# A two-layer mixture-of-experts model on one core: the router multiplies the residual itself, and the norm's scale moves into the router's matrix

## The chip, the cores and the metric

The kernel runs on one core of one Trainium2 chip. The metric is the device time of one launch in microseconds, the median of several executions; less is better.

## The reference, cut to what matters

There are two layers. In each, 256 tokens `x` and 256 context tokens `xc` (width 1024) go through a token mixer and then through a hierarchical mixture of 32 experts. The second layer computes the context only as far as the mixer of `x` needs it, so its experts see 256 tokens, the first layer's 512.

```
mod = c_act @ w_mod[i] + b_mod[i]
sh1, sc1, g1, sh2, sc2, g2 = split(mod, 6)
x = x + g1 * mix
x = x + g2 * hierarchical_moe(rms_norm(x, norm2_g) * (1 + sc2) + sh2, ...)

def hierarchical_moe(t, ...):
    group_p, group_idx = top_k(softmax(t @ w_group + b_group), 1)
    sel_logits = (t @ w_expert + b_expert)[the 8 experts of that group]
    top_val, top_idx = top_k(sel_logits, 2)
    top_w = softmax(top_val) * group_p
    y = sum over the two experts of top_w * (silu(t @ w1[e]) * (t @ w3[e])) @ w2[e]
```

`rms_norm(x, g)` is `x * rsqrt(mean(x*x) + 1e-6) * g`. The group's 4 logits and the experts' 32 are one product of width 36.

## The kernel before

Tokens lie in tiles of 128 rows: four in layer 0 (two sides, `x` and `xc`, of two tiles each), two in layer 1. Each layer runs `mixers`, whose last product is `mix` (matmuls `pmix`, three passes of split operands; DVE multiplies by the gate, `prm`/`prl`, and adds to the residual `x`), and then `moe` (L1442 on).

**Router.** For each tile `moe` squares `x` on ACT with a sum (`sq`), DVE makes `rnv`, POOL takes the power -1/2 (`rn`, L347), DVE multiplies and adds (`h = x*rn*G2 + sh2`, two passes of 1024 columns), POOL writes `h` to DRAM (`h2d`, L1461), PE transposes `h` in two groups of four (`pth`, L1466), ACT copies them (`h2T`). For each pair of tiles PE makes the logits (`plg`, 16 fp32 matmuls) and turns them back (`plt`, L1482), and DVE adds the bias (`lg`).

```
for i, t in enumerate(tiles):
    r = self.square(tp, self.x[t // 2][:, t % 2])
    self.stt(h, self.x[t // 2][:, t % 2], r, self.G2[t // 2], OP.mult, OP.mult)
    self.add(h, h, self.sh2[t // 2])
    self.G.dma_start(hd[i * 128:(i + 1) * 128], h)
```

`route` then ranks on DVE in some fifty small operations, with one round of small matmuls (`prk`) that counts the tokens of each expert. In `experts`, `look` multiplies one-hot rows by token numbers (`pvi`), `place` makes addresses (`ix`, `at`), and `fetch` gathers the token rows of a quad of four experts from `h2d` with an indirect DMA issued by POOL (`xg`, L1741). `count` makes the number of tokens that overflow a slot (`k`), which DVE loads into a register for the branch at L1972 and L1973 (`If(v > done)`, not entered for these inputs). The tiles of `route`, `weigh` and `learn` come from the experts' pool `ep`, which takes the memory of the router's own tiles.

**Experts.** 32 experts in 8 quads. Of a quad, `gather` transposes the fetched rows (`pgt`, L226), `first` multiplies by W1 and W3 (`pab`), `hidden` makes silu and product and transposes (`pat`), `second` multiplies by W2 in two column halves (`pye`, then ACT and DVE split the result, `yy`), and `combine` adds back to the tokens (`pcb`, then DVE `pg`, L195, and `x`, L198). Each quad needs 12 weight pieces of 1 MB, loaded by SP's queue (L340); 9 are loaded ahead in layer 0 and 16 in layer 1, the others as buffers come free. While a quad is in `hidden` and `second`, steps of the quad before's `combine` and of the next quad's `gather` lie between, at places set in the loop from L1999 on. `self.line` chains PE's matmuls in the order written.

**The next layer's modulation.** `mod_steps` multiplies the activations by eight 1 MB pieces of `w_mod` (`pm`, four matmuls for each piece, three buffers), adds the bias (`w<-w,pm`), transposes (`ptm`) and copies (`modT`). For layer 1 the first of its three parts runs inside layer 0's router, eight steps ahead of the routing's matmuls.

Elsewhere each engine's order is that of a scheduler that follows the program's order and the operations' readiness.

Of the kernel before, what the change touches and what calls it, by code (L numbers as in the profile page):

```python
# [19 lines left out]
D = 1024  # L20
# [157 lines left out]
class Net:  # L178
    def __init__(self, tc, A, out, dbg=None, stop=None):
        self.tc, self.nc, self.A, self.out = tc, tc.nc, A, out  # L180
        self.dbg, self.stop = dbg, stop
        self.line = None
        self.V, self.S, self.G, self.T, self.Y = (tc.nc.vector, tc.nc.scalar, tc.nc.gpsimd, tc.nc.tensor,
                                                  tc.nc.sync)
# [43 lines left out]
    def queue(self, i):  # L228

        if self.line is not None:  # L230
            ins = getattr(i, "ins", i)
            for last in self.line:
                self.tc.add_manual_dep(ins, last.name, mybir.DependencyInfo(mybir.DependencyClass.NoSync,
                                                                            mybir.DependencyReason.DATA), reason="line")
            self.line = [ins]
        return i

    def mm3(self, o, lh, ll, rh, rl, start, stop):
# [46 lines left out]
    def consts(self):  # L285
# [37 lines left out]
        self.bg = None  # L323
        self.modT = [cp.tile([128, 16, 2], F32, name=f"modT{l}") for l in range(L)]
        self.dmod = [self.dp.tile([2, 128, 512], F32, name=f"dmod{l}") for l in range(L)]

# [24 lines left out]
    def mod_steps(self, l, b):  # L351

        pm = self.pm(name="pm")
        for k in range(8):
            w = self.weight(self.A["wmod"][l, b, k])
            for q in range(4):
                self.mm(pm[32 * q:32 * q + 32, :], self.actp[:, k, :], w[:, q * 512:(q + 1) * 512], k == 0, k == 7,
                        tile_position=(0, 32 * q))
            if k < 7:
                yield  # L360
        w = self.slot()
        bt, R, nt = w[:, 0:512], w[:, 512:1024], w[0:64, 1024:1536]
# [4 lines left out]
        self.add(R, bt, pm)  # L367
        if b == 0:
            pt = self.ax(name="ptm")
            for j in range(4):  # L370
                self.T.transpose(pt[:, j * 128:(j + 1) * 128], R[:, j * 128:(j + 1) * 128], self.ident)
            mT = self.modT[l]
            pv = pt.rearrange("p (j q s) -> p q j s", j=4, q=4)[:, :, :, 0:2]
            mq = mT.rearrange("p (q j) s -> p q j s", q=4)
            self.V.tensor_copy(mq[:, 0:2], pv[:, 0:2])
            n1 = self.P["n1"].rearrange("p (l q j) -> p l q j", l=L, q=2)[:, l]
            self.stt(mq[:, 2:4, :, 0], pv[:, 2:4, :, 0], 1.0, n1, OP.add, OP.mult)
            self.stt(mq[:, 2:4, :, 1], pv[:, 2:4, :, 1], 1.0, n1, OP.add, OP.mult)
        else:
# [5 lines left out]
            self.G.dma_start(self.dmod[l][b - 1], R)  # L385
        yield

# [1026 lines left out]
    def moe_open(self, l):  # L1414
# [21 lines left out]
        self.V.tensor_copy(self.tri, self.cst["tri"])  # L1436
        ss = range(self.T0 // 256, 2)
        self.G2 = {s: self.vec(self.rb, l, "G2", s, tag="rb") for s in ss}
        self.sh2 = {s: self.vec(self.rb, l, "sh2", s, tag="rb") for s in ss}

    def moe(self, l):
# [6 lines left out]
        with ExitStack() as cx:  # L1448
# [4 lines left out]
            with tc.tile_pool(name=f"rl{l}", bufs=2, reuse_waits="tile") as tp:  # L1453
                hs, hTs, lT = [], [], None
                for i, t in enumerate(tiles):
                    r = self.square(tp, self.x[t // 2][:, t % 2])
                    h = tp.tile([128, D], F32, name="h2", bufs=NT)
                    self.stt(h, self.x[t // 2][:, t % 2], r, self.G2[t // 2], OP.mult, OP.mult)
                    self.add(h, h, self.sh2[t // 2])
                    hs.append(h)  # L1460
                    self.G.dma_start(hd[i * 128:(i + 1) * 128], h)  # L1461
                    hT = tp.tile([128, 8, 128], F32, name="h2T", bufs=3)
                    for kh in range(2):
                        pt = self.ax(name="pth2")
                        for k in range(4):
                            self.T.transpose(pt[:, k * 128:(k + 1) * 128],  # L1466
                                             h[:, (4 * kh + k) * 128:(4 * kh + k + 1) * 128], self.ident)
                        self.copy(hT[:, 4 * kh:4 * kh + 4], pt.rearrange("p (k t) -> p k t", k=4))
                    hTs.append(hT)
                    if i % 2 == 0:  # L1470
                        lT = tp.tile([128, 128], F32, name="lT")
# [3 lines left out]
                    for k in range(8):  # L1475
                        for u in range(2):
                            self.mm(pl[64 * u:64 * u + 36, 0:128], self.wr[:, k], hTs[i - 1 + u][:, k], k == 0, k == 7,
                                    tile_position=(0, 64 * u))
# [19 lines left out]
    def route(self, rp, l, lg, NT, R):  # L1498
# [39 lines left out]
        Mf = M[1:]  # L1538
        pk = self.ax(name="prk")
        H = PARTS[l]  # L1540
        hn = NT // H
# [128 lines left out]
    def experts(self, l, ep, R, more, later, hd, NT, NTOK, tiles):  # L1670
# [40 lines left out]
        def place(qd, v):  # L1711
# [6 lines left out]
            g["at"] = ep.tile([128, nb], I32, name="at")  # L1718
            self.add(g["at"], g["ix"], e)

# [123 lines left out]

        def first(qd):

# [3 lines left out]
            for k in range(8):  # L1850
# [7 lines left out]
                for b in range(g["nb"]):  # L1858
                    for e in range(n):
                        self.mm(ps[b][32 * e:32 * e + 32], g["xT"][k // 4][:, k % 4, b, e], w[e], k == 0, k == 7,  # L1860
                                tile_position=(0, 32 * e))

        def hidden(qd):
# [33 lines left out]
        def second(qd):  # L1897
# [4 lines left out]
            for hf in range(2):  # L1902
# [5 lines left out]
                for b in range(g["nb"]):  # L1908
                    ws = g["ws"][:, b:b + 1]
                    py = self.sx(name="pye")[0:n]  # L1910
                    for c in range(2):
# [7 lines left out]
                    g["y"][hf, b] = yy  # L1919
                yield  # L1920

# [37 lines left out]

        self.line = []  # L1960
        for qd in range(2):
            prepare(qd)
            place(qd, look(qd, self.tok4, 4, "pvi")[:, :, 0])
            if qd == 0:
                fetch(0)
                go(later)
        more(ep)
        self.line = None
# [22 lines left out]
        first(0)  # L1991
        self.learn(ep, NT, R)
        if not self.last:
            self.spread(ep, l, NT, R, "sm")
        for qd in range(2):
            worth(qd, look(qd, R["val"][:, :, qd, 4:12], 8, "pvw"))
        ex = none()
        for qd in range(nq):
# [4 lines left out]
            if qd + 2 < nq:  # L2003
                prepare(qd + 2)
            if qd > 0:
# [5 lines left out]
            com = combine(*([qd - 1] + (["x"] if qd - 1 == x_at else []))) if qd > 0 else none()  # L2011
            gat = gather(qd + 1) if qd + 1 < nq else none()
# [14 lines left out]
            out = second(qd)  # L2027
            go(out, 1)
            xout = second("x") if qd == x_at else none()
# [59 lines left out]
```

## Time and profile before

| | us |
|---|---|
| median of 3 runs | 1653.12 |
| lowest, highest | 1651.6, 1655.12 |
| the profiled run's own time | 1651.6 |
| its span, first to last instruction | 1649.7 |
| PE busy | 1493.0 (91%) |
| DVE busy | 959.2 (58%) |
| ACT busy | 534.6 (32%) |
| POOL busy | 83.7 (5%) |
| mean granted clock of TensorE | 0.964 |
| moved from HBM | 380.81 MB, 239 GB/s over the span |

PE, DVE, ACT and POOL are the engines for matmuls, vectors, activations and the rest; SP issues the weight loads. "Idle before, <- X" in a row is the time an engine stood before an instruction and what released it. PE's fp32 matmuls are recorded as two passes, so 16 of them show as x32; transposes show once. Granted clock 1.00 is 2.4 GHz and 0.50 is 1.2 GHz.

### The profile page before, as it was taken

The page shows a single profiled execution, that of the slowest core. Times are in us where ns is not written, and L with a number is a line of the kernel's source. Part 1 is how long each engine was busy: PE and PEld are TensorE (multiplying, and loading weights), DVE is VectorE, ACT ScalarE, POOL GpSimd, SP SyncE. Part 2 cuts the span into 40 slices and gives each one's busy share as a digit, 9 for nine tenths or more (in the row PEclk, how much of TensorE's full clock was granted, in tenths as well). Part 3 has the DMA queues.
Part 4 walks back from the last instruction along what each step waited for, and adds up shares of the span by engine and source line. Part 5 has one row for each costly group of instructions (what it writes and reads, how often), then busy time and mean ns, then how long its engine had stood idle before and what let it go on. Part 6 is the DMA issues. An engine that isn't in the chain of part 4 may idle for free.

```text
span 1649.7 us, 26481 instructions
## 1 busy us (share of the span) xinstructions
PE 1493.0 (91%) x10595; PEld 969.3 (59%) x10595; DVE 959.2 (58%) x2252; ACT 534.6 (32%) x1044; POOL 83.7 (5%) x110
## 2 busy tenths in 40 slices
PE   4899999999998999699979989999999995998885
PEld 2566755687886797344444446686889893333221
DVE  7788997655475554445343466696576753233324
ACT  3423434342253322022111224244455531222211
POOL 1000000000000001101000000000000102000000
PEclk9899999999999999799989998999999997999998
DMA  7533254431221497899999954548624388999995
GB/s 284 191 117 130 93 204 147 165 138 52 89 91 52 135 342 255 275 387 386 386 339 392 387 208 180 209 165 304 214 78 154 92 291 310 373 381 382 379 380 194
DMA packets 147772, 384.81 MB, mean 233 GB/s; under 512 B 10167, under 2 KB 15863, under 8 KB 135612
## 3 DMA queue, kind: packets, MB, share of 16 engines
q1 hardware_dynamic: 140204, 367.65, 61.7%
q0 software_dynamic: 6864, 13.06, 2.4%
q10 hardware_dynamic: 576, 2.36, 0.5%
q8 instruction: 85, 1.39, 0.3%
q14 instruction: 43, 0.35, 0.1%
HBM read 380.81 MB, written 12.81 MB: 239 GB/s over the span
## 4 chain that ended last, share of the span: by engine, by line
PE 35%; DVE 8%; DMA 7%; issue 4%; ACT 3%; SPq 1%; POOL 1%; POOLq 0%; DVEq 0%; ACTq 0%
PE pab L223 9%; PE pye L223 7%; PE pcm L223 6%; PE pcb L223 4%; DMA w<-in_w_dram 4%; PE pbr L223 1%; PE pgt L226 1%; DVE wl L201 1%; DVE zz L209 1%; PE pmix L223 1%; ACT xT L215 1%; DMA w<-in_winc_dram 1%; PE pm L223 1%; PE po L223 1%; ACT wh L215 1%
## 5 line engine op out<-in xcount | busy, mean ns | idle before, releaser
L223 PE MATMUL pcm<-hh,wh 128*128 128x512 f32 (+1 forms) x736 | 262.4, 357 | 2.7 <-ACT wh L215 2.7
L223 PE MATMUL pcm<-hh,wl 128*128 128x512 f32 (+1 forms) x736 | 257.6, 351 | 1.6 <-DVE wl L201 1.6
L223 PE MATMUL pcm<-hl,wh 128*128 128x512 f32 (+1 forms) x736 | 258.7, 352 | 0.2 <-DVE hl L201 0.2
L223 PE MATMUL pab<-w,xT 128*32 128x512 f32 x2048 | 230.6, 594 | 19.9 <-DMA w<-in_w_dram 19.8
L201 DVE TENSOR_TENSOR wl<-w,wh 128x1024 fp32r<-128x1024 f32 x128 | 155.5, 1222 | 127.0 <-ACT wh L215 120.8
L215 ACT ACTIVATE wh<-w 128x1024 fp32r<-128x1024 f32 x128 | 134.5, 1057 | 246.9 <-PE pcm L223 164.5
L223 PEld LDWEIGHTS pab<-w,xT 128*32 128x32 f32 x2048 | 63.6, 110 | 181.6 <-issue 134.6
L223 PEld LDWEIGHTS pcm<-hh,wh 128*128 128x128 f32 x736 | 140.9, 192 | 35.1 <-issue 10.2
L223 PEld LDWEIGHTS pcm<-hh,wl 128*128 128x128 f32 x736 | 140.4, 191 | 22.3 <-issue 4.8
L223 PEld LDWEIGHTS pcm<-hl,wh 128*128 128x128 f32 x736 | 140.9, 191 | 18.3 <-issue 2.9
L209 DVE SCALAR_TENSOR_TENSOR th<-th,pab 128x256 f32<-128x256 f32 (+1 forms) x33 | 13.9, 421 | 233.2 <-ACT th L212 233.2
L223 PE MATMUL pye<-w,aT 128*32 128x512 f32 x1024 | 119.8, 609 | 3.5 <-ACT xT L215 3.5
L223 PE MATMUL pcb<-yy,oT 128*128 128x512 f32 x320 | 95.3, 426 | 3.1 <-DVE pg L195 1.6
L212 ACT ACTIVATE th<-pab 128x256 f32<-128x256 f32 (+1 forms) x33 | 12.6, 383 | 237.9 <-PE pab L223 229.4
L209 DVE SCALAR_TENSOR_TENSOR yy<-pye,ws,yy 128x512 fp32r<-128x512 f32 x64 | 48.0, 750 | 65.5 <-ACT yy L212 65.4
L223 PE MATMUL ptk<-wh,hh 128*128 128x256 f32 x288 | 82.8, 287 | 0.0
L223 PE MATMUL ptk<-wh,hl 128*128 128x256 f32 x288 | 82.7, 287 | 0.0
L223 PE MATMUL ptk<-wl,hh 128*128 128x256 f32 x288 | 82.3, 286 | 0.0
L223 PEld LDWEIGHTS pcb<-yy,oT 128*128 128x128 f32 x320 | 56.8, 194 | 42.4 <-issue 16.9
L212 ACT ACTIVATE yy<-pye,ws 128x512 fp32r<-128x512 f32 x64 | 44.0, 687 | 114.1 <-PE pye L223 114.1
L223 PE MATMUL pm<-w,actp 128*32 128x512 f32 x384 | 72.1, 625 | 6.2 <-DMA w<-in_wmod_dram 6.2
L195 DVE TENSOR_TENSOR pg<-g,pcb 128x512 f32<-128x512 f32 x96 | 64.8, 684 | 21.5 <-PE pcb L223 20.0
(405 smaller groups left out, 2535.9 us busy)
## 6 DMA issues: line engine op xcount, KB each, us to landing
w<-in_w_dram SPq DMA_DIRECT2D x198, 1024.0 KB
w<-in_wmod_dram SPq DMA_DIRECT2D x48, 1024.0 KB
w<-in_winc_dram SPq DMA_DIRECT2D x42, 1024.0 KB
w<-in_wint_dram SPq DMA_DIRECT2D x10, 1024.0 KB
w<-in_wout_dram SPq DMA_DIRECT2D x10, 1024.0 KB
w<-in_wmix_dram SPq DMA_DIRECT2D x8, 1024.0 KB
dtb<-T SPq DMA_DIRECT2D x4, 1472.0 KB
T<-dtb SPq DMA_DIRECT2D x4, 1472.0 KB
```

Of the source, the lines that this page charges most:

```text
L195: return self.V.tensor_tensor(o, a, b, op=OP.mult)
L201: return self.V.tensor_tensor(o, a, b, op=OP.subtract)
L209: return self.V.scalar_tensor_tensor(o, a, s, b, op0=op0, op1=op1)
L212: return self.S.activation(o, a, f, bias=bias, scale=scale, **k)
L215: return self.S.activation(o, a, AF.Copy, bias=0.0, scale=1.0)
L223: return self.queue(self.T.matmul(o, l, r, start=start, stop=stop, **k))
L226: return self.queue(self.T.transpose(o, a, ident))
```

## The change

Six things are done; line numbers after are those of the new file.

1. The router's transposes (`pth`, now L1501) take `x`. The norm's scale is multiplied into the router's matrix (`wrg`, one DVE operation for each side), the shift's product with the matrix becomes a bias (`brs`, 8 fp32 matmuls `pbs` for each side), and the logits are `plt * rs + brs`, one DVE operation for each tile. `h` is still made and written to `h2d`, after the transposes.
2. The squares are in two parts of 768 and 256 columns, and POOL's power writes the scale directly.
3. `mod_steps` transposes the other two parts of the modulation also (`modX`: four transposes and a copy each, twice a layer).
4. `route`, `learn` and `spread` take their tiles from the router's pool. The branch, which is not entered, now also copies the values that `learn` and `tables` read onto themselves, so their operations come behind it. Seven steps of the next layer's modulation stand ahead of `route` and the eighth behind it; the bias is added after the first `at` (`follow`).
5. In the last quad, the steps of quad 6's `combine` stand between the pieces of `first`; `second` yields after each half block, its second half lies in other PSUM buffers (`self.acc`), and the last `combine` is spread over it.
6. By the scheduler's choice, in the passage from layer 0 to layer 1 ACT's and DVE's splits of the first weight pieces (`wh`, `wl`, two each) stand ahead of the squares of the next norm.

```diff
+        for s in ss:
+            self.wrg[s] = ro.tile([128, 8, 36], F32, name=f"wrg{s}")
+            self.mul(self.wrg[s], self.wr, self.modX[l][:, 1, :, s:s + 1].to_broadcast([128, 8, 36]))
+            pb = self.ax(name="pbs")
+            for k in range(8):
+                self.mm(pb[:, 0:36], self.modX[l][:, 0, k, s:s + 1].to_broadcast([128, 128]), self.wr[:, k], k == 0, k == 7)
+            self.brs[s] = ro.tile([128, 36], F32, name=f"brs{s}")
+            self.add(self.brs[s], self.br, pb[:, 0:36])
...
-                    r = self.square(tp, self.x[t // 2][:, t % 2])
-                    h = tp.tile([128, D], F32, name="h2", bufs=NT)
-                    self.stt(h, self.x[t // 2][:, t % 2], r, self.G2[t // 2], OP.mult, OP.mult)
-                    self.add(h, h, self.sh2[t // 2])
-                    hs.append(h)
-                    self.G.dma_start(hd[i * 128:(i + 1) * 128], h)
+                    self.act(sq[:, 768:], x[:, 768:], AF.Square, accum_out=ss[:, 1, c])
+                    self.ts(ms[:, 1, c], ss[:, 1, c], 1.0 / D, ms[:, 0, c], OP.mult, OP.add)
+                    self.G.tensor_tensor(rs[:, c], ms[:, 1, c], self.mhalf[:, 0:1], op=OP.pow)
...
                             self.T.transpose(pt[:, k * 128:(k + 1) * 128],
-                                             h[:, (4 * kh + k) * 128:(4 * kh + k + 1) * 128], self.ident)
+                                             x[:, (4 * kh + k) * 128:(4 * kh + k + 1) * 128], self.ident)
...
-                    self.add(lg[:, i - 1:i + 1], pl[:, 0:128].rearrange("p (u e) -> p u e", u=2)[:, :, 0:36],
-                             self.br.rearrange("p (o e) -> p o e", o=1).to_broadcast([128, 2, 36]))
+                    for u in range(2):
+                        j = i - 1 + u
+                        self.stt(lg[:, j], pl[:, 64 * u:64 * u + 36], rs[:, j:j + 1], self.brs[t // 2], OP.mult, OP.add)
...
-            R = {"tok": self.cst["tok"]}
-            more = self.route(rp, l, lg, NT, R)
+            R = {"tok": self.cst["tok"], "pool": rp}
             later = iter(())
             if l + 1 < L:
                 later = self.mod_steps(l + 1, 0)
-                for _ in range(8):
+                for _ in range(7):
                     next(later)
+            more = self.route(rp, l, lg, NT, R)
+            next(later, None)
...
-        more(ep)
+        more(R["pool"])
...
+            for v1 in (R["w"], R["rk"], R["upto"], gb[0]["ix"], gb[1]["ix"]):
+                self.V.tensor_copy(v1, v1)
...
-                first(qd)
+                first(qd, com if qd + 1 == nq else ())
...
-            last = combine(qd) if qd + 1 == nq else none()
-            go(last, NT)
+            last = none()
+            if qd + 1 == nq:
+                last = combine(qd)
+                go(out, 1)
+                go(last, 2)
```

PE's order in layer 0's router, before, from the first step of the modulation behind the mixer (`pm`, four matmuls for each piece) on:

```order
2468 L223 MATMUL pm<-w,actp 32x512 x12
2469 L1466 MATMUL pth_5930<-ident,h_5925 128x128 x4
2470 L1466 MATMUL pth_5936<-ident,h_5925 128x128 x4
2471 L223 MATMUL pm<-w,actp 32x512
2472 L1466 MATMUL pth_5956<-ident,h_5951 128x128 x4
2473 L1466 MATMUL pth_5962<-ident,h_5951 128x128 x4
2474 L223 MATMUL plg<-h2T,wr 36x128 x16
2475 L223 MATMUL pm<-w,actp 32x512 x4
2476 L1482 MATMUL plt<-ident,lT 128x128
```

The same place now:

```order
2473 L1501 MATMUL pth_5978<-ident,x_5401 128x128 x4
2474 L1501 MATMUL pth_5984<-ident,x_5401 128x128 x4
2475 L1501 MATMUL pth_6001<-ident,x_5401 128x128 x4
2476 L1501 MATMUL pth_6007<-ident,x_5401 128x128 x4
2477 L223 MATMUL pm<-w,actp 32x512 x9
2478 L223 MATMUL plg<-h2T,wrg_5432 36x128
2479 L223 MATMUL pm<-w,actp 32x512 x3
2480 L223 MATMUL plg<-h2T,wrg_5432 36x128 x15
2481 L1501 MATMUL pth_6045<-ident,x_5402 128x128 x4
2482 L223 MATMUL pm<-w,actp 32x512
2483 L1521 MATMUL plt<-ident,lT 128x128
```

The transposes of the first pair went ahead of the modulation's first three pieces. Of the 32 matmuls `pm`, 29 stood ahead of the counting matmuls `prk` before, and 28 do now.

DVE's order in layer 1 between the second address of the first quads and the branch, before (`lt`, `val`: the routing weights; `oT`: one-hot rows for `combine`; `k`: the overflow):

```order
1850 L198 TENSOR_TENSOR at<-ix,none 128x2
1851 L195 TENSOR_TENSOR lt_13540<-r_13124,s_13236 128x64
1852 L198 TENSOR_TENSOR k_13212<-k_13210 128x32
1853 L205 TENSOR_SCALAR oT<-c_iota,ix 128x128
1854 L206 TENSOR_SCALAR k_13212<-k_13212 128x32
1855 L198 TENSOR_TENSOR lt_13539<-lt_13539,lt_13540 128x64
1856 L205 TENSOR_SCALAR k_13212<-k_13212 128x32
1857 L205 TENSOR_SCALAR oT<-c_iota,ix 128x128
1858 L205 TENSOR_SCALAR k_13212<-k_13212 128x32
1859 L1631 CAST val<-lt_13539 128x16x4
1860 L205 TENSOR_SCALAR oT<-c_iota,ix 128x128
```

The same place now:

```order
1867 L198 TENSOR_TENSOR at<-ix,none 128x2
1868 L198 TENSOR_TENSOR k_13291<-k_13289 128x32
1869 L206 TENSOR_SCALAR k_13291<-k_13291 128x32
1870 L205 TENSOR_SCALAR k_13291<-k_13291 128x32 x2
1871 L1631 SCALAR_TENSOR_TENSOR k_13298<-k_13296,k_13291 128x32
1872 L1633 CAST k_13300<-k_13298 128x1
1873 L2015 TENSOR_LOAD k_13300
1874 L2016 COMPARE_AND_BRANCH
```

Only the overflow's operations are left between the address and the branch; the others went behind it. Layer 0 has the same with more of them.

PE's order at the end of layer 1, from the last quad's first products (`pab`) on, before:

```order
4831 L223 MATMUL pab<-w,xT 32x512 x64
4832 L223 MATMUL pcb<-yy,oT 128x512 x2
4833 L226 MATMUL pat<-ident,th 128x128 x4
4834 L223 MATMUL pcb<-yy,oT 128x512 x2
4835 L223 MATMUL pye<-w,aT 32x512 x16
4836 L223 MATMUL pcb<-yy,oT 128x512 x8
4837 L223 MATMUL pye<-w,aT 32x512 x16
4838 L223 MATMUL pcb<-yy,oT 128x512 x4
```

The same place now:

```order
4853 L223 MATMUL pab<-w,xT 32x512 x8
4854 L223 MATMUL pcb<-yy,oT 128x512 x2
4855 L223 MATMUL pab<-w,xT 32x512 x8
4856 L223 MATMUL pcb<-yy,oT 128x512 x2
4857 L223 MATMUL pab<-w,xT 32x512 x32
4858 L226 MATMUL pat<-ident,th 128x128 x4
4859 L223 MATMUL pye<-w,aT 32x512 x24
4860 L223 MATMUL pcb<-yy,oT 128x512 x4
4861 L223 MATMUL pye<-w,aT 32x512 x8
4862 L223 MATMUL pcb<-yy,oT 128x512 x4
```

The eight `pcb` of the quad before went between the first products, and four of the last eight went ahead of the last `pye`.

## Rows read from the trace of the kernel before

**Rows 1.** The page's chain that ended last: share of the span by engine.

```profile
PE 35%; DVE 8%; DMA 7%; issue 4%; ACT 3%; SPq 1%; POOL 1%; POOLq 0%; DVEq 0%; ACTq 0%
```

**Rows 2.** Chain of waits, layer 1's router: start us, us, what.

```profile
1364.24 1.16 ACT sq L212 x2
...
1370.65 1.23 DVE h L198
...
1372.17 7.35 DMA h2d<-h
...
1388.80 5.01 DMA xg<-h2d,at
...
1395.89 13.11 PE pab L223 x120
```

**Rows 3.** Timeline of DVE, layer 1's router: start us, us, instruction [idle before].

```profile
1377.64 0.23 DVE L198 TENSOR_TENSOR lg<-plt,br 128x72 f32<-128x72 f32 x1 [5.76 <-PE plt L1482]
1379.65 0.09 DVE L1587 MEMSET k<- 128x32 f32 x1 [1.78 <-DMA h2d<-h]
...
1386.45 0.15 DVE L198 TENSOR_TENSOR at<-ix,none 128x2 int32<-128x2 f32 x1
```

**Rows 4.** Timeline of PE, layer 1: the mixer's end and the logits.

```profile
1350.99 0.39 PE L223 MATMUL pmix<-wl,mh 128*128 128x256 f32 x1 [2.60 <-DVE wl L201]
...
1373.89 2.70 PE L223 MATMUL plg<-h2T,wr 128*36 128x128 f32 x32
```

**Rows 5.** Windows, layer 1: us, busy PE, PEld, DVE, ACT, POOL, granted clock, DMA share, GB/s.

```profile
1385.00:1405.00 20.00, 14.14 (x110) 6.88 (x114) 3.40 (x26) 2.39 (x4) 4.10 (x4) 0.73 0.67 210
...
1500.00:1600.00 100.00, 83.49 (x684) 27.35 (x688) 31.62 (x67) 20.04 (x37) 4.88 (x5) 1.00 1.04 380
```

**Rows 6.** Timeline of PE, layer 0's router.

```profile
639.71 2.78 PE L223 MATMUL pm<-w,actp 128*32 128x512 f32 x24
644.84 1.77 PE L1466 MATMUL pth<-ident,h 128*128 128x128 f32 x8 [2.35 <-DVE h L198]
...
661.38 1.28 PE L223 MATMUL pm<-w,actp 128*32 128x512 f32 x8 [2.17 <-DMA w<-in_wmod_dram]
665.85 1.92 PE L223 MATMUL pm<-w,actp 128*32 128x512 f32 x2 [3.18 <-DMA w<-in_wmod_dram]
...
671.25 0.58 PE L223 MATMUL pvi<-tok,oh 128*128 128x4 f32 x4 [1.72 <-DVE oh L192]
...
681.78 3.81 PE L226 MATMUL pgt<-ident,xg 128*128 128x128 f32 x16 [6.47 <-DVEq L1973]
```

**Rows 7.** Timeline of DVE, layer 0's router.

```profile
660.61 0.09 DVE L1587 MEMSET k<- 128x32 f32 x1 [2.12 <-DMA h2d<-h]
...
669.81 0.69 DVE L198 TENSOR_TENSOR w<-w,pm 128x512 f32<-128x512 f32 x1 [1.01 <-DMA w<-in_bmod_dram]
```

**Rows 8.** Timeline of POOL, layer 0's router: the first gather.

```profile
674.19 1.10 POOL L1741 DMA_INDIRECT xg<-h2d,at  x1 [10.20 <-DVE oh L192]
```

**Rows 9.** Windows, layer 0, same columns as rows 5.

```profile
675.00:690.00 15.00, 8.53 (x61) 4.56 (x65) 8.69 (x44) 2.39 (x4) 3.87 (x4) 0.63 0.49 161
```

**Rows 10.** Chain of waits, layer 0's first quad: fp32 matmuls with a 128-column stationary operand.

```profile
699.66 1.88 PE pvw L223 x16
```

**Rows 11.** Timeline of PE, the end of layer 1.

```profile
1619.11 1.92 PE L223 MATMUL pab<-w,xT 128*32 128x512 f32 x16 [0.80 <-DMA w<-in_w_dram]
...
1623.82 3.64 PE L223 MATMUL pye<-w,aT 128*32 128x512 f32 x32
...
1631.49 5.31 PE L223 MATMUL pye<-w,aT 128*32 128x512 f32 x32
...
1638.90 0.51 PE L223 MATMUL pcb<-yy,oT 128*128 128x512 f32 x1 [0.79 <-DVE yy L209]
```

**Rows 12.** Timelines of PE and ACT, from layer 0 to layer 1.

```profile
986.94 1.11 PE L549 MATMUL pth<-ident,xn 128*128 128x128 f32 x4 [3.51 <-DVE rnv L206]
...
988.66 1.99 ACT L215 ACTIVATE wh<-w 128x1024 fp32r<-128x1024 f32 x2
```

More of the change, by code (lines that the diff above doesn't have):

```diff
@@ L181, in __init__ @@
         self.dbg, self.stop = dbg, stop
-        self.line = None
+        self.line, self.behind = None, None
         self.V, self.S, self.G, self.T, self.Y = (tc.nc.vector, tc.nc.scalar, tc.nc.gpsimd, tc.nc.tensor,
@@ L236, in queue, with follow @@
         return i
+    def follow(self, i, last):
+        self.tc.add_manual_dep(getattr(i, "ins", i), getattr(last, "ins", last).name,
+                               mybir.DependencyInfo(mybir.DependencyClass.NoSync, mybir.DependencyReason.DATA),
+                               reason="behind")
     def mm3(self, o, lh, ll, rh, rl, start, stop):
@@ L324, in consts @@
         self.modT = [cp.tile([128, 16, 2], F32, name=f"modT{l}") for l in range(L)]
+        self.modX = [cp.tile([128, 2, 8, 2], F32, name=f"modX{l}") for l in range(L)]
         self.dmod = [self.dp.tile([2, 128, 512], F32, name=f"dmod{l}") for l in range(L)]
@@ L366, in mod_steps @@
             yield
-        self.add(R, bt, pm)
+        i = self.add(R, bt, pm)
+        if self.behind is not None:
+            self.follow(i, self.behind)
+            self.behind = None
         if b == 0:
@@ L385, in mod_steps @@
             self.G.dma_start(self.dmod[l][b - 1], R)
+            pt = self.ax(name="ptm")
+            for j in range(4):
+                self.T.transpose(pt[:, j * 128:(j + 1) * 128], R[:, j * 128:(j + 1) * 128], self.ident)
+            pv = pt.rearrange("p (j q s) -> p q j s", j=4, q=4)[:, :, :, 0:2]
+            self.V.tensor_copy(self.modX[l][:, b - 1].rearrange("p (q j) s -> p q j s", q=2),
+                               pv[:, 2:4] if b == 1 else pv[:, 0:2])
         yield
@@ L1453, in moe @@
             with tc.tile_pool(name=f"rl{l}", bufs=2, reuse_waits="tile") as tp:
-                hs, hTs, lT = [], [], None
+                ss = tp.tile([128, 2, NT], F32, name="ss", bufs=1)
+                ms = tp.tile([128, 2, NT], F32, name="ms", bufs=1)
+                rs = tp.tile([128, NT], F32, name="rs", bufs=1)
+                early = slice(0, 768)
                 for i, t in enumerate(tiles):
-                    r = self.square(tp, self.x[t // 2][:, t % 2])
-                    h = tp.tile([128, D], F32, name="h2", bufs=NT)
-                    self.stt(h, self.x[t // 2][:, t % 2], r, self.G2[t // 2], OP.mult, OP.mult)
-                    self.add(h, h, self.sh2[t // 2])
-                    hs.append(h)
-                    self.G.dma_start(hd[i * 128:(i + 1) * 128], h)
+                    sq = tp.tile([128, D], F32, name="sq")
+                    self.act(sq[:, early], self.x[t // 2][:, t % 2, early], AF.Square, accum_out=ss[:, 0, i:i + 1])
+                    self.ts(ms[:, 0, i:i + 1], ss[:, 0, i:i + 1], 1.0 / D, EPS, OP.mult, OP.add)
+                hTs, lT = [], None
+                for i, t in enumerate(tiles):
+                    x = self.x[t // 2][:, t % 2]
+                    c = slice(i, i + 1)
+                    sq = tp.tile([128, D], F32, name="sq")
+                    self.act(sq[:, 768:], x[:, 768:], AF.Square, accum_out=ss[:, 1, c])
+                    self.ts(ms[:, 1, c], ss[:, 1, c], 1.0 / D, ms[:, 0, c], OP.mult, OP.add)
+                    self.G.tensor_tensor(rs[:, c], ms[:, 1, c], self.mhalf[:, 0:1], op=OP.pow)
                     hT = tp.tile([128, 8, 128], F32, name="h2T", bufs=3)
@@ L1539, in route @@
         pk = self.ax(name="prk")
+        self.line = []
         H = PARTS[l]
@@ L1718, in place @@
             g["at"] = ep.tile([128, nb], I32, name="at")
-            self.add(g["at"], g["ix"], e)
+            return self.add(g["at"], g["ix"], e)
         def worth(qd, v):
@@ L1843, in borrow, with first @@
             return w
-        def first(qd):
+        def first(qd, beside=()):
             g = gb[qd]
@@ L1861, in first @@
                                 tile_position=(0, 32 * e))
+                next(iter(beside), None)
         def hidden(qd):
@@ L1909, in second @@
                     ws = g["ws"][:, b:b + 1]
-                    py = self.sx(name="pye")[0:n]
+                    py = (self.acc if qd == nq - 1 and hf else self.sx)(name="pye")[0:n]
                     for c in range(2):
@@ L1919, in second @@
                     g["y"][hf, b] = yy
-                yield
+                    yield
         def combine(*qds):
@@ L1957, in experts @@
             ready[k] = self.weight(quarter(*k), self.yy)
-        self.line = []
         for qd in range(2):
             prepare(qd)
-            place(qd, look(qd, self.tok4, 4, "pvi")[:, :, 0])
+            i = place(qd, look(qd, self.tok4, 4, "pvi")[:, :, 0])
             if qd == 0:
                 fetch(0)
+                self.behind = i if l + 1 < L else None
                 go(later)
-        more(ep)
+        more(R["pool"])
         self.line = None
@@ L1991, in experts @@
         first(0)
-        self.learn(ep, NT, R)
+        self.learn(R["pool"], NT, R)
         if not self.last:
-            self.spread(ep, l, NT, R, "sm")
+            self.spread(R["pool"], l, NT, R, "sm")
         for qd in range(2):
@@ L2004, in experts @@
                 prepare(qd + 2)
+            com = combine(*([qd - 1] + (["x"] if qd - 1 == x_at else []))) if qd > 0 else none()
             if qd > 0:
@@ L2027, in experts @@
             out = second(qd)
-            go(out, 1)
+            go(out, 2)
             xout = second("x") if qd == x_at else none()
```

10 lines of the change are left out of this document (7 added, 3 removed).

## The prediction

> **What bounds the kernel now.** I read the chain of waits first. PE has 35% of it, DVE 8%, DMA 7% [rows 1]; the chain shows which work is followed in each stage, so I looked at the stages that the edits touch, in their timelines.
>
> The router of layer 1 is a serial stretch. The chain there goes squares, power, two DVE passes for h, the write of h to DRAM (7.35 us), routing, the gather (5.01 us) and only then the first `pab` at 1395.89 [rows 2]. The point to see: DVE had the logits at 1377.64 + 0.23 = 1377.87, yet the first operation on them starts at 1379.65, released by the landing of h2d [rows 3]. Routing does not read h2d; its tiles lie in memory that the router's own tiles, h among them, held. Meanwhile the weight stream runs dry: between 1385 and 1405 the DMA share is 0.67 [rows 5]. Against the 1.04 of a full stream [rows 5] this is (1 - 0.67/1.04) x 20 = 7.1 us of lost transfer time, because all buffers are full and only `pab` frees them. From there to the end the stream is the limit: in the window from 1500 to 1600 the share is 1.04 and PE works 83.49 of 100 us, and the last `pab` rows wait for DMA w [rows 5, 11]. So what layer 1's router gives is kept at the end only if the stream restarts earlier, and it is at most 7.1 us.
>
> Layer 0's router has the same shape, with other covers. PE fills the wait for h with the modulation's products, then waits twice for pieces of w_mod (2.17 and 3.18 us), then 1.72 us for DVE, and the first `pgt` starts at 681.78 after 6.47 us of waiting for DVE's branch [rows 6]. The stream is thin there as well: share 0.49 over 675 to 690, 7.9 us lost by the same working [rows 9].
>
> At the end of layer 1 the last `pab` row ends at 1621.03, and then 64 recorded `pye` passes, sixteen `pcb` and their DVE steps follow until the last `pcb` at 1638.90 (1636.80, where the last `pye` ends, is 1631.49 + 5.31) [rows 11].
>
> **The change, part by part.**
>
> *Bias products `pbs`.* Per side 8 fp32 matmuls, 16 passes, with a 128-column stationary operand. The nearest rows are `pvw`, 16 such passes in 1.88 us, 0.1175 each [rows 10]. Layer 0 gets 32 passes, 3.8 us, amid `pmix`, on PE's busy stretch, and I choose to let 0.6 of it fall into `pmix`'s short waits: +3.2 on the mixer's end. Bounds: 32 x 0.084 = 2.7 less 0.6, 2.1, by `plg` (2.70 us for 32 passes [rows 4]), and 32 x 0.24 = 7.6, by `pgt` at the half clock, 3.81 for 16 [rows 6]. I take `pvw`, the same form. Layer 1 has 16 passes, 1.9 us; `pmix` waits 2.60 us for `wl` just there [rows 4], so I cost it at nothing; without that cover it is +1.9.
>
> *Layer 0's router.* The transposes no longer wait for h (2.35 us [rows 6]), but three pieces of the modulation now stand behind 16 transposes, so the buffers of w_mod come free later. Routing starts with the logits, not with h2d (2.12 us [rows 7]). Net of the +3.2 I put routing's start some 4 us earlier. What decides is when piece 7 of w_mod lands, since `pvi` stands behind it in both kernels: 665.85 before [rows 6]. The wait for the bias (1.01 us [rows 7]) goes behind the first address, and routing's earlier end removes the 1.72 us before `pvi`. I put the gather at 670 instead of 674.19 [rows 8]. The branch then has only the overflow's operations ahead of it, so the 6.47 us before `pgt` [rows 6] are bounded by the gather's landing: `pgt` at about 677.5, **-4**. Bounds: piece 7 three microseconds later, +1; all 7.9 us of the lost stream, -8.
>
> *`modX`.* Four groups of four transposes. `pgt` gives 3.81/16 x 4 = 0.95 each at the half clock, about half of that at the full one; sum 1.9 to 3.8, some of it in waits for pieces. I take **+1** (0 to +3.8). The copies lie on DVE, which waits for PE there.
>
> *Layer 0 to layer 1.* Last `combine` steps earlier in layer 0 shorten nothing large, as PE is the limit there. The two `wh` of 1.99 us now run ahead of the next squares, in ACT's idle time, if the weights have landed; the first transposes wait 3.51 us on the norm [rows 12]. I take **-1.5** (-4 if all of the 3.51 and part of the `wh` goes; +2 if `wh` delays the squares by its 1.99).
>
> *Layer 1's router.* Out of the path: the power's and h's passes, and the 1.78 us for h2d. Squares start with the last quarter of x, transposes at once. From `pmix`'s end near 1364.2 [rows 2]: the transposes of two tiles 3.5 (8 in 1.77 [rows 6]) and the last copy, together about 4 us, `plg` 2.7 [rows 4], copies and `plt` about 1: logits at 1372.1 instead of 1377.87, and routing begins there instead of 1379.65, 7.5 earlier. Routing itself takes 1386.45 - 1379.65 = 6.8 [rows 3], so the address comes at about 1379. The gather also needs h2d, whose second write still ends near 1372.17 + 7.35 = 1379.5 [rows 2]: it goes out at 1380 to 1381 instead of 1388.80 (its second half). It lands in 5.01 us [rows 2], but perhaps while prefetching is still running, as the stream goes dry only after 1385. I add 1.5 for that. `pab` then starts at about 1389.5 instead of 1395.89: **-6** with 0.4 kept back (-3 if the landing takes twice 5.01; -7.1 is the lost stream).
>
> By the Trainium skill, "DMA: Bandwidth & Descriptors", section "Issuing engines are not separate DMA queues", transfers of SP and of GpSimd run on the same 16 engines and interleave, so an early gather would share them with the prefetch. The trace agrees in kind, as h2d took 7.35 us under a full stream and the gather 5.01 with a thin one; by that rule alone the gather would take some 7.35 and this term would be -5.
>
> *End of layer 1.* `pab` still ends when the stream does. The eight `pcb` of quad 6 and their DVE steps go into the gaps before it (0.80 us for each piece [rows 11]). From 1621.03: the wait for the last gate product and `pat`, until about 1623.2; 32 `pye` (64 recorded), of which 32 took 3.64 us: 7.28; four `pcb` between, 1.2; then ACT and DVE split the last part, 1.4 (before it was 1638.90 - 1636.80 = 2.1 [rows 11] with one multiplication of some 0.7 between), and the last `pcb` starts at 1633.1. If 32 of them are again as slow as the second 32 were (5.31, 1.67 more [rows 11]) it is 1634.8. I take 1634.4, **-4.5** (-3 to -6). The steps behind it are as before.
>
> Sum: -4 + 1 - 1.5 - 6 - 4.5 = -15. The span goes from 1649.7 to 1634.7, the profiled run from 1651.6 to 1636.6. The median of the runs was 1653.12, 1.5 above the profiled one: **1638.1** for the median. The lower ends together would be -25 and the upper ones +1, or +5 with the dear `pbs`, but they do not come together.
>
> **Rivals.**
>
> *The stream absorbs the routers.* Both earlier `pab` starts are lost because the gathers meet the full stream, or because buffers come free at the same times. For it: the stream bounds all of the second half of layer 1 [rows 5]. Against it: it stands thin for 7.1 and 7.9 us [rows 5, 9], waiting for `pab`. Then only the end, the passage and modX count: -5, **1648**.
>
> *Layer 0 gives nothing.* Piece 7 of w_mod lands late, since 16 transposes and `pbs` stand ahead of the first `pm`, and its 4 us go. For it: the two DMA waits of PE there [rows 6]. Against it: the later pieces' buffers came free behind `plg`, which now comes earlier. **1642**.
>
> *Slower: a late piece of w_mod.* PE's queue keeps its order, and in layer 0 everything behind piece 7 waits for it. The loads of pieces 3 to 7 are issued only as the first `pm` rows free their buffers. If those start after the dear `pbs` (7.6) and after 16 transposes (3.5 [rows 6]) and their copies (about 2), piece 7 lands up to 13 later; 1.72 of slack stood before `pvi` [rows 6], so the gather and `pab` come 11.3 later instead of 4 earlier. With layer 1's earlier gather waiting for the stream likewise (0 for -6) the sum is 11.3 + 1 - 1.5 - 4.5 = +6: **1659**. It decides at a landing 10 us after 665.85: 5 that the rest gives, 3.3 that can be told, and the slack. Against it: the first transposes wait no longer for h, 2.35 [rows 6], and pieces 6 and 7 were held by buffers freed behind `plg`.
>
> *The change does not take routing off h2d.* If some tile of routing still waits for h's landing, layer 1 gives 1.8 less from h2d's earlier issue, about -4 there: **1640**, inside the range.
>
> **How the numbers follow.** The sum, with or without the small loss of the last rival, 0.62. Layer 0 gives nothing, 0.15. The stream absorbs, 0.15, of which 0.05 lies so near the old time that it counts as no change. The late piece of w_mod, 0.08: slower 0.05, and 0.03 where it only cancels the rest. A measurement of this kernel can tell about 0.2%, 3.3 us, from no change. Faster by more: 0.62 + 0.15 + 0.10 = 0.87; within it 0.05 + 0.03 = 0.08; slower 0.05. The range: the sum's terms vary by 2 to 3 us each, about 5 together, and 3 more if layer 0 recovers all of its lost stream, so 1630 below; above it takes in layer 0 giving nothing and the absorbed stream: 1648.
>
> **What would show it.** Right: layer 1's first routing operation follows `plt` without a wait for h2d, near 1372 less what came earlier; `pab` 6 us earlier after the mixer's end; the thin window of the stream shorter by as much; `pgt` in layer 0 released by the gather, not by DVE's branch; and four to five microseconds less from the last `pab` to the last `pcb`. Wrong: piece 7 of w_mod landing later than before, gathers of over 8 us, a dry stream of the same length, or ACT's `wh` with a wait for DMA ahead of the next squares.

## The result, and the profile after

The changed kernel takes **1665.13 us** (median of 5 runs, 1661.6 to 1667.08), the kernel before 1653.12 in the same comparison: a ratio of 1.0071, 95% interval 1.0055 to 1.0087. It is slower by 12 us, where 15 less was forecast. The profiled run's span is 1663.2 instead of 1649.7.

The spans of both profiled runs, cut at the same marks of PE and POOL (us; each is a difference of two starts or ends in the timelines):

| stretch | before | after | |
|---|---|---|---|
| start to layer 0's first `pmix` | 592.6 | 592.1 | -0.5 |
| layer 0: first to last `pmix` | 47.2 | 64.8 | **+17.6** |
| layer 0: last `pmix` to the first gather's issue | 34.4 | 32.8 | -1.6 |
| layer 0: gather's issue to the first `pab` | 11.3 | 10.9 | -0.4 |
| layer 0: first `pab` to last `pcb` | 297.9 | 299.0 | +1.1 |
| to layer 1's first `pcm` | 14.9 | 15.8 | +0.9 |
| layer 1: `pcm` to the last `pmix` | 365.9 | 363.9 | -2.0 |
| layer 1: last `pmix` to the first `pab` | 31.6 | 27.9 | -3.7 |
| layer 1: first to last `pab` | 225.2 | 230.0 | +4.8 |
| layer 1: last `pab` to last `pcb` | 18.4 | 15.7 | -2.7 |
| to the end | 10.3 | 10.4 | +0.1 |

One row is larger than the whole difference: the first mixer. The prediction had +3.2 for it, the bias products, and at the dearest 7.6. PE's timeline of the changed kernel there shows one wait of more than a microsecond:

```profile
609.90 7.01 PE L223 MATMUL pbs<-wr,modX 128*128 128x36 f32 x32 [7.58 <-DMA wr<-in_wr_dram]
```

The new bias products waited 7.58 us for the router's matrix `wr`, and then 32 passes took 7.01 us, 0.219 each. Layer 1's products, with PE busy before them, give the price at the full clock:

```profile
1359.42 1.87 PE L223 MATMUL pbs<-wr,modX 128*128 128x36 f32 x16
```

That is 0.117 a pass, what the prediction took from `pvw` [rows 10]. The windows of the mixer show what clock layer 0's products had (us, busy PE, PEld, DVE, ACT, POOL, granted clock, DMA share, GB/s):

```profile
592.10:602.30 10.20, 8.69 (x66) 8.09 (x66) 8.16 (x9) 3.96 (x4) 1.55 (x3) 1.00 0.97 328
602.30:609.90 7.60, 0.01 (x2) 0.03 (x1) 0.37 (x2) 0.00 (x0) 2.22 (x5) 0.80 1.01 302
609.90:616.90 7.00, 7.00 (x33) 7.00 (x34) 0.91 (x3) 0.00 (x0) 0.00 (x0) 0.50 0.13 47
616.90:627.00 10.10, 10.10 (x73) 10.10 (x72) 4.04 (x13) 1.06 (x1) 0.00 (x0) 0.82 0.13 29
```

While PE stood idle the granted clock fell to its lower level, 0.50 (1.2 GHz), and all of `pbs` ran there; some `pmix` behind it too. The wait and the passes make 14.6 of the 17.6 us, ten microseconds at 0.82 another 1.8 by my estimate (10.1 x 0.18), and two new waits of 0.76 us of `pmix` for `ml` most of the rest. The last two rows show more: SP's weight loads are held by the same stop (it waits 22.5 us for DVE's `wl` there), so the stream carried 29 to 47 GB/s for 17 us.

Why was `wr` late? POOL's timeline before, and after:

```profile
538.34 0.60 POOL L1424 DMA_DIRECT2D wr<-in_wr_dram  x1 [0.16 <-DVE prod L209]
```

```profile
600.75 0.60 POOL L1441 DMA_DIRECT2D wr<-in_wr_dram  x1 [63.30 <-DVE ml L201]
```

The load was issued 62.4 us later. It waits for DVE to have made `ml`, an operand of the mixer's last products. I read from this that the memory that `wr` now has was the mixer's until then; experiment 1 tests it. `wr` is the first tile of the router's constant pool, and the change adds `wrg` and `brs` to that pool. It also landed late, in a full stream (the answer for the tile `wr`, both layers):

```profile
DMA to landing us min/median/max: 2.4/5.7/9.0
```

The 9.0 is layer 0's, in a window of DMA share 1.01. In the kernel before both loads landed in 2.5 us, and nothing needed them before the logits.

The lines that answer to the rows of before: in layer 0's router PE's timeline now reads

```profile
679.96 1.94 PE L223 MATMUL pm<-w,actp 128*32 128x512 f32 x8 [6.36 <-DMA w<-in_wmod_dram]
...
684.17 1.94 PE L223 MATMUL pm<-w,actp 128*32 128x512 f32 x8 [1.90 <-DMA w<-in_wmod_dram]
...
696.83 3.80 PE L226 MATMUL pgt<-ident,xg 128*128 128x128 f32 x16 [4.51 <-DVE val L201]
```

PE stands 6.36 us for piece 6 of w_mod ahead of `prk`, where it stood 2.17 [rows 6]. Piece 7 came 26.1 us after the mixer's end (665.85 less 639.7) and now comes 27.5 after it (684.17 less 656.7). The wait ahead of `pgt` is shorter than the 6.47 of before and is the gather's: issued at 689.67, it landed 7.02 us later, 0.1 before `pgt`. DVE's name in the row is only the semaphore that came last. In the kernel before the gather was nearly as binding: issued at 674.19 [rows 8], it landed 6.97 us later, 0.6 before `pgt`, so the branch held little there.

In layer 1 the logits are ready 9.1 us after the mixer's end instead of 13.7, routing follows them at once (at 1388.41, 0.04 later) without a wait for h2d, and the chain reads (start us, us, what)

```profile
1395.99 7.33 DMA xg<-h2d,at
1403.45 3.79 PE pgt L226 x16
1407.24 14.08 PE pab L223 x120
```

against a gather of 5.01 us [rows 2]. That one is the second of the two that `pgt` needs; like for like the first took 4.18 us before and 7.33 now, the second 5.01 and 7.68. While the first was on its way the DMA share was 0.39 before and is 1.05 now. SP's waits in that stretch (us in total, times, longest) have two new ones:

```profile
SPq L2016 <- SPq L2016: 11.7, 4, 4.5
SPq L422 <- DVE lg L209: 9.8, 1, 9.8
```

SP loads the gate `g2` into memory that the router's first tiles held. Before, that memory was free after the squares (SP's wait there was 3.5 us, for ACT's `sq`); now the norm's root lies in it and is read by the logits. The weight pieces behind this load in SP's queue wait too. The other wait, at the branch, follows from it: SP stands there for the semaphores of the four pieces that it has just issued, until they have landed. Before, those pieces had gone out earlier and SP's wait of this kind was 0.5 us; what held it then was first the branch's value (11.0 us for DVE's `oT`), where the prediction had full buffers alone. So the first piece behind the branch went out 5.1 us ahead of the first `pab` before, and goes out 3.0 behind it now: one piece of 1 MB less lies ready.

The end of layer 1, on PE:

```profile
1635.24 1.92 PE L223 MATMUL pab<-w,xT 128*32 128x512 f32 x16 [0.79 <-DMA w<-in_w_dram]
...
1640.63 3.74 PE L223 MATMUL pye<-w,aT 128*32 128x512 f32 x32 [0.51 <-DMA w<-in_w_dram]
1645.97 1.06 PE L223 MATMUL pye<-w,aT 128*32 128x512 f32 x8 [1.60 <-DMA w<-in_w_dram]
...
1652.33 0.49 PE L223 MATMUL pcb<-yy,oT 128*128 128x512 f32 x1 [0.76 <-DVE yy L209]
```

There two of the last weight pieces are now waited for, 0.51 and 1.60 us, where the work of `combine` covered them before [rows 11].

### The profile page after: what moved, and what is told of

It is laid out like the page before. It is cut to its first block, busy times and chain, and to the rows that moved or that the text cites. A ratio compares the mean times of both kernels' runs of the same rounds, so it can differ in the third digit from the quotient of the medians.

```text
span 1663.2 us, 26646 instructions
## 1 busy us (share of the span) xinstructions
PE 1501.1 (90%) x10659; PEld 973.2 (59%) x10659; DVE 964.7 (58%) x2271; ACT 536.0 (32%) x1056; POOL 84.0 (5%) x110
## 4 chain that ended last, share of the span: by engine, by line
PE 33%; DMA 9%; DVE 8%; issue 4%; ACT 3%; SPq 1%; POOL 1%; POOLq 0%; DVEq 0%; ACTq 0%
PE pab L223 9%; DMA w<-in_w_dram 7%; PE pcm L223 7%; PE pye L223 6%; PE pcb L223 4%; DVE wl L201 1%; PE pbr L223 1%; PE pgt L226 1%; DVE zz L209 1%; PE pm L223 1%; DMA w<-in_winc_dram 1%; SPq L347 1%; PE po L223 1%; ACT xT L215 1%; DVE pg L195 1%
## 5 line engine op out<-in xcount | busy, mean ns | idle before, releaser
L223 PE MATMUL pab<-w,xT 128*32 128x512 f32 x2048 | 234.4, 598 | 20.2 <-DMA w<-in_w_dram 20.1
L223 PEld LDWEIGHTS pcm<-hh,wh 128*128 128x128 f32 x736 | 139.7, 190 | 35.5 <-issue 10.9
```

Of the source, the lines that this page charges most:

```text
L223: return self.queue(self.T.matmul(o, l, r, start=start, stop=stop, **k))
```

## The experiments

### 1. The matrix back in its place

```diff
+        ss = range(self.T0 // 256, 2)
+        self.wrg = {s: ro.tile([128, 8, 36], F32, name=f"wrg{s}") for s in ss}
+        self.brs = {s: ro.tile([128, 36], F32, name=f"brs{s}") for s in ss}
         self.wr = ro.tile([128, 8, 36], F32, name="wr")
...
-            self.wrg[s] = ro.tile([128, 8, 36], F32, name=f"wrg{s}")
...
-            self.brs[s] = ro.tile([128, 36], F32, name=f"brs{s}")
```

> The change with one edit: the tiles wrg and brs are taken from the router's constant pool ahead of wr, so that wr lies where it lay in the kernel before. Theory A (the loss is made in layer 0's mixer: the larger pool puts wr on memory that the mixer frees late, wr is loaded 62 us later, and PE, which needs it only now for pbs, stands 7.6 us for it and then runs pbs at the half clock, 7.0 us): the load of wr goes out near 538 instead of 600.75, PE's wait for it is gone, pbs takes about 3.8 us in layer 0, and the time falls by 12 to 14 us, to about 1652. Theory B (pbs itself, or what else stands on PE there, is the cost, and the late load only hides it): the time falls by under 4 us, 1661 or more.

1652.17 us, a ratio to the kernel before of 1.0006 (0.9990 to 1.0022). Nothing but the order of the tiles in a pool was changed, every engine runs the same instructions, and 13 us of the median are gone (11 by the two ratios). This run is wr_place below; its executions spread from 1648.63 to 1659.82, so a few microseconds of a single profile say little about a median. POOL issues the load where it did before:

```profile
538.67 0.60 POOL L1444 DMA_DIRECT2D wr<-in_wr_dram  x1 [0.16 <-DVE prod L209]
```

PE's waits have none for `wr`, and the first mixer takes 51.6 us, 4.4 more than before, of which `pbs` is 3.65 at the full clock:

```profile
602.97 3.65 PE L223 MATMUL pbs<-wr,modX 128*128 128x36 f32 x32
```
Theory A is shown for the loss. But in the medians the kernel that is left is no faster than the one before, so the gains are missing too.

### 2. Without the bias products

```diff
-            pb = self.ax(name="pbs")
-            for k in range(8):
-                self.mm(pb[:, 0:36], self.modX[l][:, 0, k, s:s + 1].to_broadcast([128, 128]), self.wr[:, k], k == 0, k == 7)
...
-            self.add(self.brs[s], self.br, pb[:, 0:36])
+            self.V.tensor_copy(self.brs[s], self.br)
```

> The change without the 8 matmuls pbs of each side; the shift's product with the router's matrix is left out of the bias, which is copied alone. wr still lies where it is loaded late. Theory A with PE alone as the one that waits: all of the loss and the cost of pbs are gone, about 1648. Theory A with DVE also held by wr (the product wrg stands in DVE's queue ahead of prm): PE loses what the mixer waits for DVE instead, and the time is between 1651 and 1656. Theory B: 1661 or more, as PE's other additions cost the time.

1659.24 us, 1.0042 (1.0026 to 1.0059): 3 us above theory A's dearer range, the one with DVE held, and 2 below theory B's bound, so no value of the expectation was met. The rows decide for A with DVE held. PE no longer needs `wr` in the mixer, but DVE does, and its queue keeps its order. DVE's waits there, then PE's:

```profile
DVE wrg L195 <- DMA wr<-in_wr_dram: 6.8, 1, 6.8
```

```profile
PE pmix L223 <- DVE wl L201: 4.8, 1, 4.8
```

The late load reaches PE by a second way: `wl`, a weight split that `pmix` needs, stands behind `wrg` on DVE. The first mixer takes 55.6 us without any `pbs`, 8.4 more than before. In the ten microseconds from 617 to 627, around the end of PE's wait, the mean granted clock was 0.66, which the expectation had not counted.

### 3. The larger pool alone, in the kernel before

```diff
+        for s in range(self.T0 // 256, 2):
+            t = ro.tile([128, 9, 36], F32, name=f"room{s}")
+            self.V.memset(t, 0.0)
         self.tok4 = ro.tile([128, 4, 4], F32R, name="tok4")
```

> The kernel before with its router's constant pool made larger by as much as the change makes it (two tiles of 128 by 324 numbers in layer 0, one in layer 1, set to zero by DVE and read by nobody). Theory A: wr is loaded late here too, near 600, but nothing needs it before the logits at 650, so the time stays within 0.2% of 1653. A rival, that the larger pool itself costs time by other waits on reused memory: 3 us or more above the kernel before.

1658.26 us, 1.0033 (1.0017 to 1.0049). The expectation of theory A, no change, was wrong; the rival's came out, 3 us or more by other waits on reused memory. `wr` was late as expected, at 600.01, and no instruction of the mixer waited for it. The other constants come behind it in POOL's queue, and DVE casts one of them early:

```profile
DVE tok L1437 <- DMA c_tok<-in_tok_dram: 8.3, 1, 8.3
```

```profile
PE pmix L223 <- DVE wl L201: 4.7, 1, 4.7
```

So 2.6 KB a partition in a pool cost 5 us of a kernel that does not use them.

### 4. The end alone, in the kernel before

The edit is part 5 of the change, with nothing else of it.

> The kernel before with only the fifth part of the change, the new order at the last quad of each layer. From the two profiles: from the last pab to the last pcb 15.2 us instead of 17.9 in layer 1, so -2.7 us there, and about +1 in layer 0: -2 us in all, 1651. If the end of layer 1 is set by the landing of the last weights instead, as the wait of 1.6 us ahead of a pye in the changed kernel's end suggests: within 1 us of the kernel before.

1649.5 us, 0.9982 (0.9971 to 0.9994): 3 us faster. From the last `pab` to the last `pcb` it takes 15.7 us instead of 18.4, as in the changed kernel. The waits of 0.53 and 1.60 us for the last pieces are here as well, so both expectations had a part: the order helps, until the last piece is late.

### 5. The gate's load not held

```diff
-                ss = tp.tile([128, 2, NT], F32, name="ss", bufs=1)
-                ms = tp.tile([128, 2, NT], F32, name="ms", bufs=1)
-                rs = tp.tile([128, NT], F32, name="rs", bufs=1)
+                ss = rp.tile([128, 2, NT], F32, name="ss")
+                ms = rp.tile([128, 2, NT], F32, name="ms")
+                rs = rp.tile([128, NT], F32, name="rs")
```

> The run wr_place with one edit more: the sums of squares and the norm's root (ss, ms, rs) are tiles of the pool that outlives the router's loop, so that the load of the gate g2, which takes the memory of the router's first tiles, waits for the squares as before, not for the logits. Theory C (layer 1's router gained 3.6 us and lost them again up to the last pab, because SP stood 9.7 us for the logits ahead of that load, and the pieces behind it then ran beside the gather, which landed in 7.3 us instead of 5.0): SP's wait for lg is gone, the gather of layer 1 lands about 2 us sooner, the stretch from the first to the last pab of layer 1 is 1 to 3 us shorter, and the time falls by 2 to 3 us against wr_place, to about 1649.5. Theory D (the weight stream alone sets the end of layer 1 and takes back any earlier start): within 1 us of wr_place.

1651.72 us, 0.9999 (0.9990 to 1.0009). SP's wait for `lg` is gone, and the stretch from the first to the last `pab` is 225.8 us, where wr_place has 228.3 and the changed kernel 230.0. The first piece behind the branch goes out just ahead of the first `pab` again. But the gather still takes 7.31 us in the chain, so its slowness does not come from the held queue, and 2.5 us of one profile are not seen in the medians: the ratios of this run and of wr_place overlap. Theory C has its wait right and one of its two effects; what it is worth in time stays open below some 2 us.

### 6. The modulation's steps first

```diff
                 early = slice(0, 768)
+                later = self.mod_steps(l + 1, 0) if l + 1 < L else iter(())
+                for _ in range(7):
+                    next(later, None)
...
-            later = iter(())
-            if l + 1 < L:
-                later = self.mod_steps(l + 1, 0)
-                for _ in range(7):
-                    next(later)
```

> The run wr_place with one edit more: the seven steps of the next layer's modulation are written ahead of the router's loop, so that PE's order in layer 0 has the fourth piece of w_mod inside the first logits instead of behind the second ones. Theory E (layer 0's router is held by pieces 6 and 7 of w_mod, whose loads wait for buffers that the fourth and fifth pieces free): PE's wait of 5.8 us for w_mod ahead of prk shrinks to under 2, the gather goes out 3 to 5 us earlier after the mixer's end, and the time falls by 3 to 4 us, to about 1648.5. Rival F (routing on DVE, or the transfers beside the stream, hold the gather anyway): 1 us or less.

1648.26 us, 0.9982 (0.9967 to 0.9997), 4 us under wr_place by both medians and ratios, though the two intervals just touch. PE's wait for w_mod ahead of `prk`, 5.8 us in wr_place, is not among its waits any more; `prk` now waits for DVE's routing:

```profile
PE prk L223 <- DVE r L195: 4.5, 1, 4.5
```

The first gather goes out 29.1 us after the mixer instead of 31.9 (34.4 before). Theory E holds for the wait, a little under the expected 3 to 5 us in the place; the time agrees with it as far as the medians can tell.

### 7. A cheaper bias

```diff
+        pb = self.ax(name="pbs")
+        for k in range(8):
+            self.mm(pb[0:2, 0:36], self.modX[l][:, 0, k, 0:2], self.wr[:, k], k == 0, k == 7)
+        bs = ro.tile([2, 36], F32, name="bs")
+        self.copy(bs, pb[0:2, 0:36])
...
+            self.mm(pb[:, 0:36], self.ident[0:2, s:s + 1].to_broadcast([2, 128]), bs, True, True)
```

> The run wr_place with one edit more: the shift's product with the router's matrix is made once for both sides with a stationary operand of two columns (8 matmuls), copied, and spread over the partitions by one small matmul for each side: 20 passes instead of 32 in layer 0, 16 of them with two columns. Theory G (pbs on PE's busy mixer costs its own time, 0.117 us a pass): layer 0's mixer, 51.6 us in wr_place and 47.2 in the kernel before, gets 1.5 to 2.5 us shorter, and the time with it, to about 1650. Rival H (the extra time of the mixer is waits of the constants or of DVE, not the passes): no change over 1 us.

1651.49 us, 0.9999 (0.9986 to 1.0012). In the profile the products take 0.68 us for 16 passes of two columns and 0.63 for the four that spread them, and the first mixer 49.8 us instead of 51.6, inside the 1.5 to 2.5 that were expected:

```profile
602.59 0.68 PE L223 MATMUL pbs<-wr,modX 128*2 128x36 f32 x16
...
603.75 0.63 PE L223 MATMUL pbs<-bs,ident 2*128 2x36 f32 x4
```

In the medians it can't be told from wr_place, so the expected effect on the time is not shown.

### 8. The three together

The three edits of experiments 5 to 7 on top of experiment 1.

> The run wr_place with the three edits of g2_early, steps_first and bias_cheap together. If theories C, E and G hold and add up: 7 to 9 us under wr_place, about 1644, faster than the kernel before by 0.5%. If the stream takes the gains back: 1649 to 1652.

**1646.86 us**, 0.9967 (0.9954 to 0.9979): 4.7 us under the kernel before in the same comparison (1651.52), 18 under the change as it was made (17 by the two ratios), and the lowest median of all, though its interval overlaps with those of experiments 4 and 6. It is between the two expectations. Experiment 4 alone gave 3 us, so what the two routers add in time is some 2 us and not clear of the noise. The first mixer has 50.0 us, the gather of layer 0 goes out after 28.6, layer 1's first `pab` after 28.1, and from there to the last `pab` it takes 225.6: in this profile, what the change won in layer 1's router is now kept.

## Why the prediction was wrong

It was wrong in its first term, the bias products `pbs`. With "amid `pmix`, on PE's busy stretch" and "+3.2 on the mixer's end" it priced the passes, and the price was right: 0.1175 forecast from `pvw`, 0.117 measured in layer 1, and 3.65 us for layer 0's 32 where `wr` is in place (experiment 1 has 4.4 more in that mixer, with 0.6 of new waits). The step that failed was not written down: that the operand is there. The wait for it was put at nothing, and it measured 7.58 us. The row for the load of `wr` in the kernel before, at 538.34, would have said yes for that kernel; but the change also adds two tiles to the pool in which `wr` is first, and pools here share memory with a mixer that is still running. Wait and half-clock passes took 14.6 us where 3.65 were due, and experiment 1 shows that it is the tile's place. The dear end of the bounds, 7.6, lies near the 7.01 that `pbs` itself took, and its reason, the half clock, was right, but the wait during which the clock fell was missing.

*Layer 0's router*, forecast -4 with the bias's +3.2 in it, so about -7 behind the mixer's end: -2.0 there. What I said decides did decide. Pieces 6 and 7 of w_mod came late, as in the rival "layer 0 gives nothing", because the fourth piece's buffer was freed only behind the second logits. I had argued against that rival that the logits come earlier; they did, but the rest of the fourth piece stood behind the first pair's logits before and stands behind the second pair's now. Experiment 6, with the pieces first, has the gather out 29.1 us after the mixer's end, where the kernel before had 34.4 and the changed one 32.8.

*Layer 1's router*, forecast -6: -3.7 up to `pab`. The logits came 4.6 us sooner than before (9.1 for 13.7 after the mixer), not 5.8: on DVE they stand behind the passes of `h` of both tiles. The first gather went out 6.5 us sooner after the mixer (16.7 for 23.2), not 8, and took 7.33 us, not 6.5. For the gather the prediction had weighed the rule of the Trainium skill, "DMA: Bandwidth & Descriptors", section "Issuing engines are not separate DMA queues", that transfers of SP and GpSimd interleave on the same engines. The runs agree: the first gather of layer 1 took 7.3 to 7.6 us in the seven kernels with the new router and 4.2 to 4.3 in the three with the old one, and the 7.35 us put down by that rule were nearer than 6.5. The 4.8 us that were lost again up to the last `pab` are the rival "the stream absorbs the routers", by a way that I did not see: SP's queue held 9.8 us behind the load of `g2`, and then at the branch. In experiments 5 and 8, without the wait for the logits, this stretch is nearly as short as before (225.8 and 225.6 for 225.2); in the five others with the new router it is 227.1 to 230.0.

*End of layer 1*, forecast -4.5: -2.7 here and in experiment 4. The order works; the term left out that `pye` then needs its own weight pieces sooner, and PE waits 0.5 and 1.6 us for two of them.

*modX*, forecast +1: no stretch that holds it is longer (start to mixer -0.5, layer 1's mixer -2.0), but the first of these stretches lasted between 591.0 and 600.6 us in the ten profiles, so this pair can't tell +1 from 0. *Layer 0 to layer 1*, forecast -1.5: +0.9 in this profile and between 13.0 and 15.8 us in the other runs for 14.9, so it is inside what one profile can tell.

The slower rival was right in the sign and wrong in the place: it too had a queue that keeps its order behind a late transfer, but it named w_mod. Even with the three repairs of experiment 8 some 10 of the 15 us forecast did not come; the stretches of one profile, which add up to more than the medians show, don't settle where each of them went.

## What to carry to other kernels

Before a new reader of an operand is priced, find the row where that operand lands, and ask whether the change itself moves it: a tile added to a pool moves its neighbours onto other memory, and a load waits for what lived there. Then list everything that stands behind the new reader on its engine, since an in-order queue carries one late load to engines that never use it. A gain ahead of a saturated stream was kept here only where the queue that issues the stream wasn't held by the same edit, and a branch counts among what can hold it, though it is not entered.

## What the runs showed of the hardware that was not expected

The load of `wr`, 128 rows of 288 numbers, landed in 2.5 us with a thin stream (DMA share 0.20 from 536 to 541 in the kernel before) and in 9.0 with a full one (1.01 in the changed kernel). And one stop of 7.6 us on PE cost about 5 us more behind it, in the two stretches with mean granted clocks of 0.50 and 0.82 shown above: 3.4 in `pbs` (7.01 instead of 3.65) and, by the estimate above, 1.8 in the ten microseconds of `pmix` that follow. At the branch, which is not entered, SP stood until the four pieces that it had issued last had landed: 11.7 us in the changed kernel, 0.5 before.
